# A hybrid decoder layer with product-key experts: ScalarE's reads of finished sums are put behind its casts, and three PSUM pools change size

## The chip, the cores and the metric

The kernel runs on one core of one Trainium2 chip. The metric is device microseconds (us) of one execution; before the change it is 3959.79 us, the median of three runs (3953.78 to 3965.73).

## The reference

One decoder layer of width 2048 for 512 tokens: two mixers side by side, then a feed-forward stage of experts. Nearly everything that the change touches lies in the experts:

```python
def one_block(xb):                                    # PEER_BLOCK tokens
    q = (xb @ w_query).reshape(PEER_BLOCK, 8, 2, 128)
    s = einsum('lhpd,hpnd->lhpn', q, sub_keys)
    s_half, i_half = top_k(s, 16)                     # 16 of 128 keys in each half
    ...                                               # 16x16 candidates, the best 16 of them
    gates = softmax(top_s)
    u = u_emb[eidx]                                   # 128 experts of 16384 for a token
    act = gelu(einsum('ld,lhkd->lhk', xb, u))
    return einsum('lhk,lhkd->ld', gates * act, v_emb[eidx])
```

The layer adds this, times a gate, to its input and ends with an RMS norm. Inputs and result are float32.

## The kernel before, in words

The mixers, their projections and the choice of experts take the first 1595 us. The experts take the rest, in two ways at once.

**Dense, for tokens 0 to 319** (`TD`). All 16384 experts are computed, and a table of gates is zero for those a token did not choose. `expert_u(i)` (L1158) computes 128 experts' scores: two pieces of 8 weight tiles go through `project_to` (L352), then ScalarE reads the finished sum `mm` from PSUM with a Gelu into `act` (L1162). `expert_g(grp)` (L1174) multiplies four of these by their gates on VectorE (L1188). `expert_v(grp)` (L1207) multiplies by the second table, in eight pieces with two sums `po` each, which VectorE adds into `hT` (L1228). There are 128 u's and 32 groups of v's.

**Gathered, for tokens 320 to 511** (`TG`). GpSimd's indirect DMA (`gather`, L1246) fetches each token's 128 rows of either table. VectorE multiplies and sums the u rows (`use`, L1259, L1263). The v rows are summed on TensorE by `part()` (L1274), here called a gathered sum: four matmuls into one PSUM tile `pw` (L1277), which ScalarE copies to `ys` (L1280) and a DMA of SyncE stores.

Float32 products are made of three matmuls (`mm3`, L204): high by high (L205), high by low (L206), low by high (L207). `split` (L199) makes the two parts of a piece: ScalarE casts the high part (L201; tiles `whi`, `vhi`, `ghi`), and GpSimd or VectorE subtracts it for the low part (L202; `wlo`, `vlo`, `glo`). The pieces of u and v share five raw buffers and three buffers each of high and low parts. So ScalarE has two kinds of work in one queue that is served in order: casts, which GpSimd and TensorE wait for, and reads of PSUM (Gelu, `ys`), which wait for TensorE.

From 1595 to 2003 us the gate table is made as well (`gate_block`, L1133): ten blocks of eight quarters. For a quarter VectorE makes `J` (L1140), VectorE and ScalarE make four `I` (L1146, L1149, L1150), TensorE multiplies them into a bank of `pg` (L1151), ScalarE copies the bank to `gb` (L1152). A block's eight copies fill the one buffer `gb`, which a 2 MB DMA stores.

PSUM has eight banks. From 1595 us on: `pu` (sums `mm`) 2, `pw2` (`pw`) 1, and 5 for `pg`, later for `pv` (sums `po`).

The order of the instructions is set when the program is built. The Python code emits them, a scheduler that simulates the engines then chooses an order by priority and readiness, and `tc.issue_after(x)` adds that what is emitted inside comes after instruction x. `pace` (L1194) uses this to space the gathers; a finished gather's `part` waits in the list `parts` until `project_to` or `expert_v` takes one between its matmuls.

Of the kernel before, what the change touches and what calls it, by code (L numbers as in the profile page):

```python
# [10 lines left out]
F32 = mybir.dt.float32  # L11
# [3 lines left out]
AF = mybir.ActivationFunctionType  # L15
OP = mybir.AluOpType
PSUM = bass.MemoryType.PSUM
DRAM = bass.MemoryType.DRAM

P = 128  # L20
T = 512
# [5 lines left out]
TD = 320  # L27
# [3 lines left out]
TF = 64  # L31
# [6 lines left out]
NSP = 36  # L38
# [98 lines left out]
def _hybrid(st, tc, nc, I, out):  # L137
    V, S, G, TE = nc.vector, nc.scalar, nc.gpsimd, nc.tensor
# [54 lines left out]
    eend = cp.tile([P, 64], F32, name="eend")  # L193

    copied = []
    parts = []
    done_mm = [None]

    def split(hi, lo, src, eng=None):  # L199

        copied.append(S.copy(hi, src))  # L201
        return (eng or V).tensor_tensor(lo, src, hi.bitcast(F32), OP.subtract)  # L202

    def mm3(ps, whi, wlo, xhi, xlo, first, last):  # L204
        TE.matmul(ps, lhsT=whi, rhs=xhi, start=first, stop=False)  # L205
# [36 lines left out]
    with ExitStack() as sb:  # L242
# [116 lines left out]
        def project_to(pss, ws, xhi, xlo, ahead=(), step=4):  # L359

            nk = ws.shape[2]
            ahead = list(ahead)
            for q in range(0, nk, step):
                n = min(step, nk - q)
                for j, ps in enumerate(pss):
                    whi, wlo, last = ahead.pop(0) if ahead else load_split(ws[j], q, n)
                    for i in range(n):
                        k = q + i
                        mm3(ps, whi[:, i, :], wlo[:, i, :], xhi[k], xlo[k], k == 0, k == nk - 1)
                        if parts and i % 4 == 3:  # L370
                            parts.pop(0)()
            return last

# [9 lines left out]
        with ExitStack() as s1:  # L383
# [158 lines left out]
            for n, (kind, i) in enumerate(MAMBA):  # L542
                ps = project(mm1, (kind, i), () if n else ahead)
# [406 lines left out]
    wp = st.enter_context(tc.tile_pool(name="wx", bufs=NSPL, reuse_waits="tile"))  # L950
    nraw = NRAW
    pu = st.enter_context(tc.tile_pool(name="pu", bufs=2, space=PSUM, reuse_waits="tile"))
    pw2 = st.enter_context(tc.tile_pool(name="pw2", bufs=1, space=PSUM, reuse_waits="tile"))
    npl = st.enter_context(tc.tile_pool(name="n2", bufs=1, reuse_waits="tile"))
    nhi = [npl.tile([P, TD], F32R, name=f"n2hi{k}") for k in range(KT)]
    nlo = [npl.tile([P, TD], F32R, name=f"n2lo{k}") for k in range(KT)]
# [1 line left out]
    gt_st = ExitStack()  # L958
# [7 lines left out]
    yG = dp.tile([TG, D], F32, name="yG")  # L966
# [6 lines left out]
    with ExitStack() as s3:  # L973
# [54 lines left out]
        for h in range(8):  # L1028
            sv = qp.tile([P, 2, 4, 16], F32, name="sv")
            si = qp.tile([P, 2, 4, 16], F32, name="si")  # L1030
            for hf in range(2):
                if h:
                    ps = pu.tile([P, T], F32, name="mm", tag="mm")
                    query([ps], 2 * h + hf)
                else:
                    ps = pss[hf]
# [72 lines left out]
        for src, dst in ((iall, iT), (jall, jT), (gall, gT)):  # L1109
            ps = pq.tile([P, 4, P], F32, name="sc")  # L1110
            for tt in range(4):
                TE.transpose(ps[:, tt, :], src[:, tt, :], ident)
            ps = ps.rearrange("p a b -> p (a b)")
# [9 lines left out]
    va = st.enter_context(tc.tile_pool(name="va", bufs=NACT, side="right", reuse_waits="tile"))  # L1123
    gr = st.enter_context(tc.tile_pool(name="gr", bufs=NGB, side="right", reuse_waits="tile"))
    gx = gt_st.enter_context(tc.tile_pool(name="gx", bufs=2, reuse_waits="tile"))
    pg = gt_st.enter_context(tc.tile_pool(name="pg", bufs=5, space=PSUM, reuse_waits="tile"))
    iota = gx.tile([P, P], F32, name="iota", bufs=1)
    G.iota(iota, pattern=[[1, P]], base=0, channel_multiplier=0, allow_small_or_imprecise_dtypes=True)

# [25 lines left out]
    acts = {}  # L1155
    actD = dp.tile([NSP, P, TD], F32, name="actD")

    def expert_u(i):  # L1158
        ps = pu.tile([P, T], F32, name="mm", tag="mm")
        last = project_to([ps[:, 0:TD]], I["uT"][i:i + 1], nhi, nlo, step=8)  # L1160
        acts[i] = va.tile([P, TD], F32, name="act")
        S.activation(acts[i], ps[:, 0:TD], AF.Gelu)  # L1162
        if i < NSP:
            nc.sync.dma_start(actD[i], acts.pop(i))
        return last

    ghl = {}
# [1 line left out]
    slots = []  # L1169
# [7 lines left out]
    def expert_g(grp):  # L1177
        gd = vp.tile([P, TD // TB, 4, TB], F32, name="gd", bufs=1)
        nc.sync.dma_start(gd, glD.rearrange("b j i t -> j b i t")[:, :, 4 * grp:4 * grp + 4, :])
        ghl[grp] = []  # L1180
        for i in range(4):
            n = 4 * grp + i
            if n < NSP:
                a = va.tile([P, TD], F32, name="act")
                nc.sync.dma_start(a, actD[n])
            else:
                a = acts.pop(n)
            V.tensor_tensor(a.rearrange("p (b t) -> p b t", t=TB), gd[:, :, i, :],  # L1188
                            a.rearrange("p (b t) -> p b t", t=TB), OP.mult)
            ghi = vp.tile([P, TD], F32R, name="ghi", bufs=7)  # L1190
            glo = vp.tile([P, TD], F32R, name="glo", bufs=7)
            split(ghi, glo, a, V)
            ghl[grp].append((ghi, glo))
# [14 lines left out]
    def expert_v(grp):  # L1208
        nonlocal nu
        gh = ghl.pop(grp)  # L1210
        for q in range(8):
            vr = wp.tile([P, 2, 4, P], F32, name="vr", tag="wr", bufs=NRAW)
            nc.sync.dma_start(vr, I["vq"][grp, q])
            vhi = wp.tile([P, 2, 4, P], F32R, name="vhi", tag="whi")
            vlo = wp.tile([P, 2, 4, P], F32R, name="vlo", tag="wlo")
            last = split(vhi, vlo, vr, G)
            po = [pv.tile([P, TD], F32, name="po") for _ in range(2)]
            for i in range(4):
                for d in range(2):
                    mm3(po[d], vhi[:, d, i, :], vlo[:, d, i, :], *gh[i], i == 0, i == 3)  # L1220
                if parts and i % 2:
                    parts.pop(0)()
            if grp == 31 and q % 2 == 0:
                sqs = vp.tile([P, 4, TD], F32, name="gd", bufs=1)
            for d in range(2):
                k = 2 * q + d
                h = hT[k]
                V.scalar_tensor_tensor(h, po[d], mod2[:, 48 + k:49 + k], h, OP.mult, OP.add)  # L1228
                if grp == 31:
                    t = sqs[:, k % 4, :] if k else sacc[:, 0:TD]  # L1230
                    S.activation(t, h, AF.Square)
                    if k:
                        V.tensor_tensor(sacc[:, 0:TD], sacc[:, 0:TD], t, OP.add)
            if q % 2 == 0:
                continue
            pace(last)
            if nu < min(128, 4 * grp + 8):
                pace(expert_u(nu))
                nu += 1
# [19 lines left out]
    def use(g, kind, i, n=None):  # L1259
# [14 lines left out]
        def part():  # L1274
            ps = pw2.tile([P, T], F32, name="pw")
            for q in range(4):
                TE.matmul(ps[32 * q:32 * q + 32, :], lhsT=wT[:, i:i + 1].to_broadcast([P, 32]), rhs=g[:, T * q:T * q + T],  # L1277
                          start=True, stop=True, tile_position=(0, 32 * q))
            ys = yp[-1].tile([P, T], F32, name="ys", bufs=len(yp))
            S.copy(ys, ps)  # L1280
            nc.sync.dma_start(yG[i].rearrange("(q n) -> q n", n=T), ys.rearrange("(q p) n -> q p n", p=32)[:, 0, :])
            held[0] -= 1
            if i % TF == TF - 1:
                late.extend((units + 2 + n, f) for n, f in enumerate(end_steps(i // TF)))

        parts.append(part)

# [49 lines left out]
    while nu < NSP:  # L1337
        pace(expert_u(nu))
        nu += 1
    gt_st.close()  # L1340
    pv = st.enter_context(tc.tile_pool(name="pv", bufs=5, space=PSUM, reuse_waits="tile"))
    vp = st.enter_context(tc.tile_pool(name="vp", bufs=2, side="right", reuse_waits="tile"))
    yp.append(vp)
    for grp in range(32):
        expert_g(grp)
        expert_v(grp)

    while slots or begun or parts or late:
        while parts:
            parts.pop(0)()  # L1350
        pace(done_mm[0])


# [30 lines left out]
```

## Time and profile before

| | |
|---|---|
| median of three runs | 3959.79 us |
| the profiled execution: its own time | 3952.57 us |
| its span | 3950.6 us |
| mean granted TensorE clock | 0.955 |
| TensorE busy | 3647.2 us, 92% |
| VectorE busy | 2431.9 us, 62% |
| ScalarE busy | 1454.1 us, 37% |
| GpSimd busy | 2429.3 us, 61% |
| DMA | 964.35 MB, mean 244 GB/s |
| chain that ended last, by engine | PE 66%, DVE 11%, POOL 7%, DMA 6%, issue 5%, ACT 1% |

PE is TensorE, DVE VectorE, ACT ScalarE, POOL GpSimd, SP SyncE. "Busy" is an average over stages that are bound by different things. "Idle before <-X" at an instruction is the time its engine stood still just before it, and X the instruction that ended that; idle time of an engine that others do not wait for costs nothing. Matmuls overlap: 0.31 us is one matmul's duration, and the distance of two starts tells the rate.

### The profile page before, as it was taken

The numbers are of one execution on the slowest core, as the hardware profiler recorded it, in microseconds if no ns is written. First come the engines' busy times: TensorE is split into PE (matmuls) and PEld (weight loads), VectorE is DVE, ScalarE is ACT, GpSimd is POOL, SyncE is SP. The second block draws the span as 40 slices with busy tenths as digits, with TensorE's granted clock in tenths as the row PEclk, the third lists the DMA queues.
The fourth block names the chain that finished last, engine by engine and source line by source line (L and its number), as shares of the span: only waits on it lengthen the run. The fifth ranks groups of instructions, "written<-read, shape, count | busy, mean of one in ns | idle before, by whom it ended". The sixth has DMA issues, their size and how long they took to land.

```text
span 3950.6 us, 61998 instructions
## 1 busy us (share of the span) xinstructions
PE 3647.2 (92%) x23708; PEld 3033.3 (77%) x23708; DVE 2431.9 (62%) x4440; ACT 1454.1 (37%) x2548; POOL 2429.3 (61%) x1393
## 2 busy tenths in 40 slices
PE   5899999999998899788979999999999999999998
PEld 3667757766666799787868788888888888788888
DVE  8543144556641699898768776657656666764225
ACT  3434323344322422565633333333333333333333
POOL 5445434433413655666647778777877887787765
PEclk8999999998888999898989999999999999999999
DMA  8465662324253422788779989898998989898884
GB/s 337 175 208 169 217 184 70 88 71 128 83 164 103 137 76 92 280 321 305 297 296 337 333 316 343 320 327 322 331 338 331 338 330 322 324 332 328 292 272 125
DMA packets 314007, 964.35 MB, mean 244 GB/s; under 512 B 67376, under 2 KB 132656, under 8 KB 257584
## 3 DMA queue, kind: packets, MB, share of 16 engines
q1 hardware_dynamic: 258416, 557.72, 42.1%
q0 software_dynamic: 55296, 402.68, 26.8%
q8 instruction: 187, 3.06, 0.3%
q14 instruction: 108, 0.88, 0.1%
HBM read 914.34 MB, written 45.94 MB: 243 GB/s over the span
## 4 chain that ended last, share of the span: by engine, by line
PE 66%; DVE 11%; POOL 7%; DMA 6%; issue 5%; ACT 1%; SPq 0%; POOLq 0%; DVEq 0%; ACTq 0%
PE mm L207 12%; PE mm L205 12%; PE mm L206 11%; PE po L207 6%; PE po L205 5%; PE po L206 5%; DVE g L1263 4%; PE pw L1277 3%; POOL vlo L202 3%; POOL wlo L202 2%; POOL g L1256 2%; DVE I L1146 2%; DMA AI<-abD 1%; PE pg L1151 1%; DVE act L1188 1%
## 5 line engine op out<-in xcount | busy, mean ns | idle before, releaser
L202 POOL TENSOR_TENSOR wlo<-wr,whi 128x1024 fp32r<-128x1024 f32 (+3 forms) x544 | 1051.5, 1940 | 797.2 <-ACT whi L201 710.2
L202 POOL TENSOR_TENSOR vlo<-vr,vhi 128x1024 fp32r<-128x1024 f32 x256 | 632.1, 2478 | 262.1 <-ACT vhi L201 257.2
L207 PE MATMUL mm<-n2hi,wlo 128*128 128x320 f32 x2304 | 732.9, 319 | 34.1 <-POOL wlo L202 33.9
L205 PE MATMUL mm<-n2hi,whi 128*128 128x320 f32 x2304 | 731.7, 318 | 11.8 <-ACT whi L201 8.4
L1263 DVE SCALAR_TENSOR_TENSOR g<-g,row 128x1024 f32<-128x1024 f32 x384 | 732.3, 1943 | 7.0 <-DMA g<-in_u,eix 3.9
L206 PE MATMUL mm<-n2lo,whi 128*128 128x320 f32 x2304 | 722.2, 314 | 0.2 <-DVE n2lo L202 0.2
L201 ACT CAST whi<-wr 128x1024 fp32r<-128x1024 f32 (+3 forms) x544 | 454.7, 840 | 671.7 <-PE mm L206 348.2
L205 PE MATMUL po<-ghi,vhi 128*128 128x320 f32 x2048 | 639.2, 317 | 35.7 <-DVE hT L1228 20.9
L206 PE MATMUL po<-glo,vhi 128*128 128x320 f32 x2048 | 637.2, 313 | 10.3 <-DVE glo L202 10.0
L207 PE MATMUL po<-ghi,vlo 128*128 128x320 f32 x2048 | 614.5, 317 | 20.9 <-POOL vlo L202 20.5
L207 PEld LDWEIGHTS mm<-n2hi,wlo 128*128 128x128 f32 x2304 | 438.4, 190 | 92.0 <-POOL wlo L202 64.0
L205 PEld LDWEIGHTS mm<-n2hi,whi 128*128 128x128 f32 x2304 | 439.9, 191 | 35.2 <-issue 18.2
L205 PEld LDWEIGHTS po<-ghi,vhi 128*128 128x128 f32 x2048 | 389.7, 191 | 83.4 <-issue 24.2
L206 PEld LDWEIGHTS mm<-n2lo,whi 128*128 128x128 f32 x2304 | 439.8, 191 | 4.2 <-issue 3.4
L1188 DVE TENSOR_TENSOR act<-gd,act 128x320 f32<-128x320 f32 x128 | 185.2, 1456 | 414.9 <-ACT act L1162 387.0
L207 PEld LDWEIGHTS po<-ghi,vlo 128*128 128x128 f32 x2048 | 380.3, 191 | 71.6 <-POOL vlo L202 45.5
L206 PEld LDWEIGHTS po<-glo,vhi 128*128 128x128 f32 x2048 | 391.2, 191 | 17.3 <-DVE glo L202 12.2
L1228 DVE SCALAR_TENSOR_TENSOR hT<-po,mod,hT 128x320 f32<-128x320 f32 x512 | 258.2, 544 | 234.6 <-PE po L207 220.6
L201 ACT CAST vhi<-vr 128x1024 fp32r<-128x1024 f32 x256 | 267.7, 1048 | 269.6 <-PE po L206 126.2
L1256 POOL DMA_INDIRECT g<-in_u,eix x192 | 237.8, 1239 | 78.3 <-issue 27.3
L1256 POOL DMA_INDIRECT g<-in_v,eT x192 | 224.8, 1171 | 70.1 <-issue 27.8
L205 PE MATMUL mm<-nhi,whi 128*128 128x512 f32 x640 | 261.8, 409 | 4.5 <-ACT whi L201 4.5
(448 smaller groups left out, 5839.6 us busy)
## 6 DMA issues: line engine op xcount, KB each, us to landing
wr<-in_uT SPq DMA_DIRECT2D x256, 512.0 KB
vr<-in_vq SPq DMA_DIRECT2D x256, 512.0 KB
wr<-in_wrest SPq DMA_DIRECT2D x160, 256.0 KB
aw<-in_ada SPq DMA_DIRECT2D x32, 1024.0 KB
a2w<-in_adar SPq DMA_DIRECT2D x64, 512.0 KB
glD<-gb SPq DMA_DIRECT2D x10, 2048.0 KB
gd<-glD SPq DMA_DIRECT2D x32, 640.0 KB
a3w<-in_adar SPq DMA_DIRECT2D x32, 512.0 KB
```

Source lines behind the costliest of these rows:

```text
L201: copied.append(S.copy(hi, src))
L202: return (eng or V).tensor_tensor(lo, src, hi.bitcast(F32), OP.subtract)
L205: TE.matmul(ps, lhsT=whi, rhs=xhi, start=first, stop=False)
L206: TE.matmul(ps, lhsT=whi, rhs=xlo, start=False, stop=False)
L207: done_mm[0] = TE.matmul(ps, lhsT=wlo, rhs=xhi, start=False, stop=last)
L1146: V.tensor_scalar(I2, iota, iT[:, t:t + 1], gT[:, t:t + 1], OP.is_equal, OP.mult)
L1151: TE.matmul(ps[:, i], lhsT=J[:, i], rhs=I2, start=True, stop=True)
L1188: V.tensor_tensor(a.rearrange("p (b t) -> p b t", t=TB), gd[:, :, i, :], a.rearrange("p (b t) -> p b t", t=TB), OP.mult)
L1228: V.scalar_tensor_tensor(h, po[d], mod2[:, 48 + k:49 + k], h, OP.mult, OP.add)
L1256: G.indirect_dma_start(out=g, out_offset=None, in_=I[s[0]], in_offset=bass.IndirectOffsetOnAxis(ap=ix, axis=0))
L1263: V.scalar_tensor_tensor(g[:, c], g[:, c], 1.0, n2s[i][:, c], OP.mult, OP.mult, accum_out=wtp[:, e, n:n + 1])
L1277: TE.matmul(ps[32 * q:32 * q + 32, :], lhsT=wT[:, i:i + 1].to_broadcast([P, 32]), rhs=g[:, T * q:T * q + T], start=True, stop=True, tile_p ...
```

## The change

Four edits, all in the experts. (1) The Gelu read and the copy to `ys` are no longer emitted at once: they go into a list `put_off`, and the next `split` whose low part is GpSimd's emits all of them, each ordered behind that split's cast. The store and the due end steps of `part` go along with its copy. The rests are emitted at the end of the gate stage, when `expert_g` needs an `act` that is missing, and in the last loop. (2) `project_to` takes a gathered sum after every eighth weight tile, not every fourth, and `expert_v` once in a piece, not twice. (3) `pw2` has two banks, not one. (4) `pg` and `pv` have four banks, not five. No instruction is added or removed; the choice of experts is as it was.

```diff
     copied = []
+    put_off = []
     parts = []
...
     def split(hi, lo, src, eng=None):
         copied.append(S.copy(hi, src))
-        return (eng or V).tensor_tensor(lo, src, hi.bitcast(F32), OP.subtract)
+        lo_ = (eng or V).tensor_tensor(lo, src, hi.bitcast(F32), OP.subtract)
+        if eng is G and put_off:
+            with tc.issue_after(copied[-1].ins):
+                while put_off:
+                    put_off.pop(0)()
+        return lo_
...
-                        if parts and i % 4 == 3:
+                        if parts and i % 8 == 7:
                             parts.pop(0)()
...
-    pw2 = st.enter_context(tc.tile_pool(name="pw2", bufs=1, space=PSUM, reuse_waits="tile"))
+    pw2 = st.enter_context(tc.tile_pool(name="pw2", bufs=2, space=PSUM, reuse_waits="tile"))
...
-    pg = gt_st.enter_context(tc.tile_pool(name="pg", bufs=5, space=PSUM, reuse_waits="tile"))
+    pg = gt_st.enter_context(tc.tile_pool(name="pg", bufs=4, space=PSUM, reuse_waits="tile"))
...
     def expert_u(i):
         ps = pu.tile([P, T], F32, name="mm", tag="mm")
         last = project_to([ps[:, 0:TD]], I["uT"][i:i + 1], nhi, nlo, step=8)
-        acts[i] = va.tile([P, TD], F32, name="act")
-        S.activation(acts[i], ps[:, 0:TD], AF.Gelu)
-        if i < NSP:
-            nc.sync.dma_start(actD[i], acts.pop(i))
+        def act():
+            acts[i] = va.tile([P, TD], F32, name="act")
+            S.activation(acts[i], ps[:, 0:TD], AF.Gelu)
+            if i < NSP:
+                nc.sync.dma_start(actD[i], acts.pop(i))
+
+        put_off.append(act)
         return last
...
             else:
+                while n not in acts:
+                    put_off.pop(0)()
                 a = acts.pop(n)
...
-                if parts and i % 2:
+                if parts and i == 3:
                     parts.pop(0)()
...
-            ys = yp[-1].tile([P, T], F32, name="ys", bufs=len(yp))
-            S.copy(ys, ps)
-            nc.sync.dma_start(yG[i].rearrange("(q n) -> q n", n=T), ys.rearrange("(q p) n -> q p n", p=32)[:, 0, :])
             held[0] -= 1
-            if i % TF == TF - 1:
-                late.extend((units + 2 + n, f) for n, f in enumerate(end_steps(i // TF)))
+
+            def out_of():
+                ys = yp[-1].tile([P, T], F32, name="ys", bufs=len(yp))
+                S.copy(ys, ps)
+                nc.sync.dma_start(yG[i].rearrange("(q n) -> q n", n=T), ys.rearrange("(q p) n -> q p n", p=32)[:, 0, :])
+                if i % TF == TF - 1:
+                    late.extend((units + 2 + n, f) for n, f in enumerate(end_steps(i // TF)))
+
+            put_off.append(out_of)
...
-    pv = st.enter_context(tc.tile_pool(name="pv", bufs=5, space=PSUM, reuse_waits="tile"))
+    pv = st.enter_context(tc.tile_pool(name="pv", bufs=4, space=PSUM, reuse_waits="tile"))
...
-    while slots or begun or parts or late:
-        while parts:
-            parts.pop(0)()
+    while slots or begun or parts or put_off or late:
+        while parts or put_off:
+            (put_off or parts).pop(0)()
         pace(done_mm[0])
```

Three places show what becomes of it in the order of the built program. The first is ScalarE's queue from the 60th Gelu of the experts on (near 2725 us before), where a gathered sum `ys`, a v piece `vhi` and a u piece `whi` meet; before:

```order
L1162 ACTIVATE act<-mm 128x320
L201 CAST ghi<-act 128x320
L1280 COPY ys<-pw 128x512
L201 CAST vhi<-vr 128x1024
L201 CAST whi<-wr 128x1024 x2
L1280 COPY ys<-pw 128x512
L201 CAST vhi<-vr 128x1024
```

and now:

```order
L1169 ACTIVATE act<-mm 128x320
L202 CAST ghi<-act 128x320
L202 CAST vhi<-vr 128x1024
L1294 COPY ys<-pw 128x512
L202 CAST whi<-wr 128x1024 x2
L1294 COPY ys<-pw 128x512
L202 CAST vhi<-vr 128x1024
```

The cast of the v piece has passed the copy of the gathered sum; the Gelu stands where it stood, with no cast moved ahead of it.

The second is TensorE's queue at the first gathered sum of the v groups (near 2031 us before), with the program's buffer numbers; `po_18851` and `po_18852` are the two sums of one piece. Before:

```order
L205 MATMUL po_18851<-ghi_18698,vhi_18847 128x320
L206 MATMUL po_18851<-glo_18699,vhi_18847 128x320
L205 MATMUL po_18852<-ghi_18698,vhi_18847 128x320
L206 MATMUL po_18852<-glo_18699,vhi_18847 128x320
L1277 MATMUL pw_18985<-g_18801,wT_11497 32x512 x2
L207 MATMUL po_18851<-ghi_18698,vlo_18848 128x320
L207 MATMUL po_18852<-ghi_18698,vlo_18848 128x320
```

and now:

```order
L211 MATMUL po_18851<-ghi_18698,vhi_18844 128x320
L212 MATMUL po_18851<-glo_18699,vhi_18844 128x320
L1288 MATMUL pw_18997<-g_18801,wT_11497 32x512 x4
L213 MATMUL po_18851<-ghi_18698,vlo_18845 128x320
L211 MATMUL po_18852<-ghi_18698,vhi_18844 128x320
L212 MATMUL po_18852<-glo_18699,vhi_18844 128x320
L213 MATMUL po_18852<-ghi_18698,vlo_18845 128x320
```

Two matmuls of the second sum no longer go ahead of the first sum's low product.

The third is ScalarE's queue in the gate stage, at the end of a block of the gate table (`whi` is the cast of a u piece, `I` the gate factors of the next block, numbered by the program). Before:

```order
L1150 ACTIVATE I_15154<-I_15154,gT,ngT 128x128
L1150 ACTIVATE I_15161<-I_15161,gT,ngT 128x128
L1149 ACTIVATE I_15172<-iota,iT 128x128
L1149 ACTIVATE I_15179<-iota,iT 128x128
L1150 ACTIVATE I_15172<-I_15172,gT,ngT 128x128
L1150 ACTIVATE I_15179<-I_15179,gT,ngT 128x128
L1152 COPY gb<-pg 128x128x4 x5
L1162 ACTIVATE act<-mm 128x320
```

and now:

```order
L1156 ACTIVATE I_15154<-I_15154,gT,ngT 128x128
L202 CAST whi<-wr 128x1024
L1155 ACTIVATE I_15161<-iota,iT 128x128
L1156 ACTIVATE I_15161<-I_15161,gT,ngT 128x128
L1169 ACTIVATE act<-mm 128x320
L1158 COPY gb<-pg 128x128x4 x4
L202 CAST whi<-wr 128x1024
L1169 ACTIVATE act<-mm 128x320
```

The copies of a block's first quarters stand together behind the store of the block before; before the change five quarters were made ahead of that point, now four (`I_15172` and `I_15179`, the fifth quarter's, come after the copies).

## Rows read from the trace of the kernel before

**Rows 1.** Windows by stage: start:end, length, busy of each engine, clock, DMA share, GB/s.

```profile
1595.00:2003.00 408.00, 355.31 (x2332) 334.16 (x2336) 334.04 (x437) 248.21 (x513) 256.81 (x128) 0.93 0.84 311
2003.00:2330.00 327.00, 293.26 (x1894) 256.33 (x1887) 258.60 (x313) 101.98 (x136) 229.99 (x122) 0.96 0.88 321
2330.00:3600.00 1270.00, 1200.84 (x7953) 1057.20 (x7952) 821.58 (x932) 416.07 (x561) 1007.83 (x526) 0.99 0.90 328
```

**Rows 2.** TensorE's waits, 2330 to 3600 us: total us, times, longest.

```profile
PE mm L207 <- POOL wlo L202: 31.5, 25, 1.6
PE po L207 <- POOL vlo L202: 19.7, 27, 3.2
PE po L206 <- DVE glo L202: 10.0, 4, 2.5
PE mm L205 <- ACT whi L201: 3.7, 9, 1.1
PE po L205 <- ACT vhi L201: 1.4, 4, 0.6
```

**Rows 3.** Timeline of ScalarE, 2724 to 2735 us: start, us, instruction, idle before.

```profile
2726.31 0.46 ACT L201 CAST ghi<-act 128x320 fp32r<-128x320 f32 x1 [0.56 <-DVE act L1188]
2728.98 0.59 ACT L1280 COPY ys<-pw 128x512 f32<-128x512 f32 x1 [2.21 <-PE pw L1277]
2729.46 1.05 ACT L201 CAST vhi<-vr 128x1024 fp32r<-128x1024 f32 x1
```

**Rows 4.** Timeline of GpSimd at the same place.

```profile
2730.59 2.37 POOL L202 TENSOR_TENSOR vlo<-vr,vhi 128x1024 fp32r<-128x1024 f32 x1 [6.44 <-ACT vhi L201]
```

**Rows 5.** Timeline of TensorE at the same place; the last row where it recurs.

```profile
2730.57 0.41 PE L205 MATMUL po<-ghi,vhi 128*128 128x320 f32 x1 [0.57 <-ACT vhi L201]
2730.96 0.31 PE L205 MATMUL po<-ghi,vhi 128*128 128x320 f32 x1
2731.11 0.31 PE L206 MATMUL po<-glo,vhi 128*128 128x320 f32 x1
2733.01 0.90 PE L207 MATMUL po<-ghi,vlo 128*128 128x320 f32 x2 [1.60 <-POOL vlo L202]
2733.71 0.47 PE L205 MATMUL po<-ghi,vhi 128*128 128x320 f32 x1
2733.98 0.47 PE L206 MATMUL po<-glo,vhi 128*128 128x320 f32 x1
...
3427.64 0.56 PE L207 MATMUL po<-ghi,vlo 128*128 128x320 f32 x2 [1.59 <-POOL vlo L202]
```

**Rows 6.** TensorE's waits, 1595 to 2003 us.

```profile
PE pg L1151 <- DVE I L1146: 32.6, 20, 4.2
```

**Rows 7.** VectorE's groups by line, 1595 to 2003 us: busy, mean ns, idle before.

```profile
L1146 DVE TENSOR_SCALAR I<-iota,iT,gT 128x128 f32<-128x128 f32 x160 | 119.4, 766 | 70.0 <-PE pg L1151 69.1
L1140 DVE TENSOR_TENSOR J<-iota,jT 128x512 f32<-128x512 f32 x79 | 63.2, 800 | 0.0
```

**Rows 8.** TensorE's waits, 2003 to 2330 us, then 3600 to 3840 us (the last row).

```profile
PE po L205 <- DVE hT L1228: 19.0, 11, 4.4
PE pw L1277 <- ACT ys L1280: 1.5, 2, 0.8
...
PE pw L1277 <- ACT ys L1280: 0.9, 1, 0.9
```

**Rows 9.** Waits of the whole span, VectorE for finished sums.

```profile
DVE hT L1228 <- PE po L207: 220.6, 133, 5.7
```

**Rows 10.** Timelines of VectorE (2355 and 2500 us on) and GpSimd: the product with the gates.

```profile
2358.61 0.48 DVE L1188 TENSOR_TENSOR act<-gd,act 128x320 f32<-128x320 f32 x1
2359.61 0.49 DVE L202 TENSOR_TENSOR glo<-act,ghi 128x320 fp32r<-128x320 f32 x1 [0.53 <-ACT ghi L201]
...
2509.19 3.40 DVE L1188 TENSOR_TENSOR act<-gd,act 128x320 f32<-128x320 f32 x1 [6.25 <-ACT act L1162]
...
2507.49 4.74 POOL L202 TENSOR_TENSOR vlo<-vr,vhi 128x1024 fp32r<-128x1024 f32 x2
```

More of the change, by code (lines that the diff above doesn't have):

```diff
@@ L1339, in _hybrid @@
         nu += 1
+    while put_off:
+        put_off.pop(0)()
     gt_st.close()
-    pv = st.enter_context(tc.tile_pool(name="pv", bufs=5, space=PSUM, reuse_waits="tile"))
+    pv = st.enter_context(tc.tile_pool(name="pv", bufs=4, space=PSUM, reuse_waits="tile"))
     vp = st.enter_context(tc.tile_pool(name="vp", bufs=2, side="right", reuse_waits="tile"))
```

## The prediction, made before the changed kernel ran

> **What bounds the kernel.** I read the windows by stage first, then TensorE's waits in each stage, then the timelines of the places where those waits lie. The windows [rows 1] say that TensorE is the bound in the experts, but not equally: in the gate stage (1595 to 2003 us) it is busy 355 of 408 us, in the first v groups 293 of 327, in the steady stage with u, v and gathers (2330 to 3600) 1201 of 1270. ScalarE, which the change is about, is busy 416 of 1270 us in the steady stage, so it has room; what can matter is only the order in which it serves its queue.
>
> What that order can cost is in TensorE's own waits of the steady stage [rows 2]: 31.5 us for `wlo`, 19.7 for `vlo`, 10.0 for `glo`, 3.7 for `whi`, 1.4 for `vhi`, together 66.3 us, 1.7% of the time. Not one of these rows ends at a DMA, although the DMA share is 0.90 [rows 1]. So 66.3 us is the most that an ideal order of casts could bring there. One place of the kind the change aims at is near 2727 us. ScalarE casts `ghi` at 2726.31, then stands 2.21 us until TensorE has a gathered sum, copies it at 2728.98, and only then, at 2729.46, casts the next v piece [rows 3]. GpSimd has stood 6.44 us for that cast and begins `vlo` at 2730.59 [rows 4]. TensorE waits 0.57 us for the cast and 1.60 us for `vlo` [rows 5].
>
> **The change, part by part.** I sum against the profiled execution's own 3952.57 us (its span is 3950.6); the median of the runs, 3959.79, is 7.2 us above it, and that is added at the end.
>
> *The later read.* The order of the built program decides what this does, and it hardly differs: a Gelu has as many casts ahead of it as before, since the scheduler had already let each read sink behind casts that were ready. At the 2727 us place the v cast now stands ahead of the copy. It can start when `ghi` ends, at 2726.77, and not at 2729.46: 2.7 us earlier, more than the 0.57 + 1.60 = 2.17 us that TensorE waits [rows 3, 5]. So I take all of 2.17 us away. The same pattern recurs once, near 3427 us, with the same 1.59 us row [rows 5]: 2 x 2.17 = 4.3. Behind the first of them the matmuls step by 0.27 us (2733.71 to 2733.98) where they stepped by 0.15 before (2730.96 to 2731.11), that is at the lower clock level after the idle time [rows 5]; nine such steps come back, 9 x 0.12 = 1.1. Elsewhere the order shows swaps of neighbours, as many for as against an earlier cast; I count them at nothing, between -33 us (half of the 66.3 gone, if ScalarE keeps ahead everywhere) and +5 us (two more places like the one removed). Nothing is near the first end in the order, so the sum takes **-5.4**.
>
> The deferral itself adds a wait: a Gelu behind a cast of 1.05 us [rows 3]. Behind it stand the gate product, `ghi` and `glo`, and the `mm` bank. I cost it at nothing, because the second `pu` bank takes the next u meanwhile; without that cover it would be 1.05 us for each of 128 u's, 134 us, but the leads in the order are unchanged, so there is nothing to cover.
>
> One rule speaks against an earlier `vlo`. The product with the gates takes 0.48 us when GpSimd stands still and 3.40 us when GpSimd is subtracting two `vlo` [rows 10], and each of the four waits for `glo` is about 2.5 us [rows 2]. The Trainium skill, "SBUF — State Buffer", section "Who interferes with whom", has the rule to it: a VectorE instruction with two inputs in SBUF contends with a GpSimd instruction that reads SBUF, and is blocked for as long as that runs. By it the two moved places would each pay 2.5 us for `glo`, and the sum would be 5.0 us higher. The rows near 2359 us, whose order on ScalarE is the one that the change brings to 2727, show `glo` done in 0.49 us [rows 10], before `vlo` starts; so I leave it out.
>
> *Fewer slots for gathered sums* move a `pw` group from the middle of a piece to its end. The four matmuls are the same. Nothing.
>
> *A second `pw` bank* removes TensorE's waits for the copy: 1.5 us in the first v groups, 0.9 at the end [rows 8]. **-2.4**. In the steady stage there is no such wait [rows 2], so nothing more.
>
> *Four banks for `po`.* The piece's second sum can start a little later. In TensorE's order two matmuls of it have stood ahead of the first sum's low products and no longer do: 2 x 0.147 = 0.29 us where TensorE waits for VectorE's addition, which it did 11 times [rows 8]: 11 x 0.29 = **+3.2**. The lower end is 0. The upper end: VectorE waited for a sum 133 times [rows 9]; the program has 256 pieces, so at up to 123 it was not ahead, 123 x 0.29 = +36.
>
> *Four banks for `pg`.* At the nine block ends of the gate stage one quarter less is made ahead. A quarter is 0.80 + 2 x 0.766 = 2.33 us of VectorE [rows 7]. VectorE is busy 334 of 408 us there and TensorE waits 32.6 us for its `I` [rows 1, 6], while VectorE waits 69.1 us for TensorE to free buffers [rows 7]: each is late for the other, so what is put off can be lost. Ends: 0, and 9 x 2.33 = +21.0. The order leaves 16 more gate matmuls, four quarters, behind the last u of the stage, 4 x 2.33 = 9.3 us of VectorE with no u beside it; but the u's stand that much earlier, so I take half, **+4.7**.
>
> Sum: -5.4 - 2.4 + 3.2 + 4.7 = +0.1. Own time 3952.7 us; against the median, **3959.9, say 3960 us: no change that can be measured**. What a measurement can tell from no change is 0.3%, 11.9 us.
>
> **The rivals.**
>
> *A, faster.* ScalarE, which is idle most of the time, uses the freedom: with the reads behind it and two `pw` banks it runs ahead of what the order suggests, and half of the 66.3 us goes, with nothing lost by the other pools. For it: the waits for `wlo` and `vlo` are 52 spread-out ones [rows 2], just what earlier casts would shorten. Against it: an engine works in its order, and that is nearly the old one. 3952.6 - 33.2 - 2.4 = 3917 own, 3924 by the median. Chance 0.18.
>
> *B, slower: the gate stage.* The lost `pg` bank costs its whole price at each block end, 21.0 in place of 4.7: 3952.6 - 7.8 + 3.2 + 21.0 = 3969 own, 3976 by the median. It decides, that is passes the 11.9 us, once over 16.5 us of the 21.0 are lost (16.5 - 7.8 + 3.2 = 11.9), at eight of nine ends. For it: both engines of that stage wait for each other [rows 6, 7]. Against it: `I` is late for want of VectorE, and a bank does not add VectorE time. Chance 0.16.
>
> *C, slower: the v pieces.* Each piece whose addition was not ahead loses its 0.29 us: 3952.6 - 7.8 + 4.7 + 36 = 3986 own, 3993 by the median. For it: 19.0 us of waits for `hT` before [rows 8]. Against it: all of them lie in 2003 to 2330 us, and the steady stage has none among its larger waits [rows 2]. The Trainium skill, "Perfetto Trace Analysis", section "Optimization Strategy", says that one gap repeating on the engine that should be saturated can mean that there isn't enough PSUM for the next tile; the trace of before shows no such gap on `po` in the steady stage with five banks, and no run here yet shows four. Chance 0.07.
>
> *D, the change does nothing:* order and waits stay, and the bank terms are nothing either; 3953 own, 3960 by the median. Chance 0.12; the time is the forecast's.
>
> **How the numbers follow.** The forecast has the remaining 0.47, of which 0.04 ends faster and 0.05 slower by over 0.3% through the ends of its own terms. Faster: 0.18 + 0.04 = 0.22. Slower: 0.16 + 0.07 + 0.05 = 0.28. Within: 0.38 + 0.12 = 0.50. The range reaches from 3936, which takes in the milder half of A, to 3988, which takes in B with the next mishap on top; left out are the stronger half of A and C, 0.16.
>
> **What would show it.** If the steps are right, the profile after has no `pw` waiting for `ys`; TensorE's 2.17 us near 2727 are gone; the steady stage's waits for casts and products sum to 58 to 67 us, against 66.3 [rows 2]; the gate stage is 0 to 9 us longer, with `pg` waiting for `I` up to 37 to 42 us; `po` waits for `hT` 20 to 24 us before 2330 and not behind it. I am wrong if the waits for `wlo` and `vlo` fall below 35 us together (A), if the gate stage is over 16 us longer (B), or if `po` waits for `hT` all through the steady stage (C).

## The result, and the profile after

The changed kernel takes 3913.84 us (median of four runs) against 3957.28 us before in the same rounds: ratio 0.9886, 95% interval 0.9867 to 0.9904, faster by 1.1%. In later rounds, beside other runs of before, it was 0.9913 (0.9894 to 0.9932). The forecast, no change, was wrong; so was its range, whose lower end was 3936. The profiled execution took 3915.02 us, its span 3912.9 us.

Where the time went is seen by cutting both spans at the same work: the end of the gate stage, the 37th Gelu of the experts and the 110th. The windows of the kernel after, columns as in [rows 1]:

```profile
1598.00:2005.00 407.00, 357.21 (x2343) 333.46 (x2344) 337.90 (x439) 249.28 (x512) 253.74 (x128) 0.94 0.84 312
2005.00:2323.00 318.00, 283.45 (x1850) 251.25 (x1850) 237.60 (x306) 100.21 (x134) 230.79 (x120) 0.96 0.90 328
2323.00:3565.00 1242.00, 1190.49 (x7973) 1053.78 (x7971) 797.54 (x937) 416.43 (x560) 1023.21 (x527) 1.00 0.91 335
3565.00:3867.00 302.00, 301.65 (x2079) 262.77 (x2078) 103.83 (x125) 111.91 (x154) 214.93 (x113) 1.00 0.80 281
```

and of the kernel before, cut at the same work:

```profile
2003.00:2325.00 322.00, 288.26 (x1860) 251.34 (x1853) 254.30 (x308) 100.15 (x133) 225.47 (x119) 0.96 0.88 322
2325.00:3598.00 1273.00, 1204.20 (x7976) 1061.58 (x7974) 824.71 (x937) 416.11 (x560) 1010.53 (x528) 0.99 0.90 328
3598.00:3905.00 307.00, 305.72 (x2083) 262.38 (x2082) 103.47 (x125) 114.62 (x155) 214.62 (x114) 1.00 0.80 277
```

The steady stage (third row above, second row here) has lost 31 us of the 37.7 by which the spans differ, with the same instructions in it; the first v groups and the last u's have each lost 4 to 5. I call "steady stage" this stretch of 73 u's from here on, 1273 us before. Of its 31 us, 17 were time in which TensorE stood still (the length less PE's busy time, 68.8 us before and 51.5 after), and 14 were busy time with the same matmuls, whose mean granted clock rose from 0.99 to 1.00. TensorE's waits in it, after:

```profile
PE mm L213 <- POOL wlo L203: 30.8, 26, 1.6
PE po L213 <- POOL vlo L203: 13.0, 17, 3.2
PE po L212 <- DVE glo L203: 4.1, 4, 1.0
PE mm L211 <- ACT whi L202: 1.8, 2, 1.3
```

Against [rows 2] the waits for `wlo`, the largest, have hardly moved. Those for `vlo`, `glo` and the casts have fallen from 34.8 to 18.9 us. VectorE's groups tell more. Before, then after (two fences, busy, mean ns, idle before):

```profile
L202 DVE TENSOR_TENSOR glo<-act,ghi 128x320 fp32r<-128x320 f32 x73 | 112.0, 1534 | 38.6 <-ACT ghi L201 35.7 <-ACT whi L201 2.9
L1188 DVE TENSOR_TENSOR act<-gd,act 128x320 f32<-128x320 f32 x73 | 100.2, 1372 | 253.5 <-ACT act L1162 244.1 <-DMA gd<-glD 9.4
```

```profile
L203 DVE TENSOR_TENSOR glo<-act,ghi 128x320 fp32r<-128x320 f32 x73 | 104.1, 1426 | 42.3 <-ACT ghi L202 42.3
L1199 DVE TENSOR_TENSOR act<-gd,act 128x320 f32<-128x320 f32 x73 | 74.9, 1026 | 226.6 <-ACT act L1169 226.6
```

The same 73 products with the gates take 25 us less of VectorE. The place where this begins is one that the prediction did not look at. Before, near 2416 us, the timelines of ScalarE, GpSimd and VectorE:

```profile
2416.28 0.59 ACT L1280 COPY ys<-pw 128x512 f32<-128x512 f32 x1 [6.04 <-PE pw L1277]
2416.77 1.05 ACT L201 CAST whi<-wr 128x1024 fp32r<-128x1024 f32 x1
...
2417.90 2.42 POOL L202 TENSOR_TENSOR wlo<-wr,whi 128x1024 fp32r<-128x1024 f32 x1 [3.81 <-ACT whi L201]
...
2422.68 4.74 POOL L202 TENSOR_TENSOR vlo<-vr,vhi 128x1024 fp32r<-128x1024 f32 x2
...
2424.37 3.41 DVE L1188 TENSOR_TENSOR act<-gd,act 128x320 f32<-128x320 f32 x1 [6.24 <-ACT act L1162]
2428.30 5.42 DVE L202 TENSOR_TENSOR glo<-act,ghi 128x320 fp32r<-128x320 f32 x1 [0.53 <-ACT ghi L201]
```

A copy of a gathered sum stands in ScalarE's queue ahead of a u piece's second cast and waits 6.04 us for TensorE. GpSimd waits 3.81 us for that cast, so its next subtractions, two `vlo`, run from 2422.7 to 2427.4. The next Gelu ends in that time, and VectorE's product takes 3.41 us in place of 0.48; `glo` then takes 5.42. After, the same work:

```profile
2407.81 1.05 ACT L202 CAST whi<-wr 128x1024 fp32r<-128x1024 f32 x1 [1.10 <-issue]
2412.75 0.59 ACT L1294 COPY ys<-pw 128x512 f32<-128x512 f32 x1 [3.89 <-PE pw L1288]
...
2408.15 4.74 POOL L203 TENSOR_TENSOR wlo<-wr,whi 128x1024 fp32r<-128x1024 f32 x2
...
2416.07 4.76 POOL L203 TENSOR_TENSOR vlo<-vr,vhi 128x1024 fp32r<-128x1024 f32 x2
...
2420.71 0.49 DVE L1199 TENSOR_TENSOR act<-gd,act 128x320 f32<-128x320 f32 x1 [5.11 <-ACT act L1169]
2422.49 2.31 DVE L203 TENSOR_TENSOR glo<-act,ghi 128x320 fp32r<-128x320 f32 x1 [1.29 <-ACT ghi L202]
```

The cast has passed the copy, the two `wlo` run without a gap, the two `vlo` are over at 2420.8, and the product takes 0.49 us. In ScalarE's order this swap ("whi, ghi, ys, whi" to "whi, ghi, whi, ys" behind a Gelu) stands at nine of the 73 u's, in twos and threes five u's apart; behind a tenth Gelu (the 77th) the cast passes the copy with `ghi` ahead of both casts.

What such a place costs depends on what TensorE needs next. Behind the one shown, the change gains 1.1 us. Behind another TensorE is at a v piece when `glo` is late: it is the place of [rows 10], with the product of 3.40 us. ScalarE's Gelus there and the matmul that waits for `glo`, before, and after with the product too:

```profile
2508.72 0.44 ACT L1162 ACTIVATE act<-mm 128x320 f32<-128x320 f32 x1 [3.27 <-PE mm L207]
2530.08 0.44 ACT L1162 ACTIVATE act<-mm 128x320 f32<-128x320 f32 x1 [5.96 <-PE mm L207]
...
2516.20 0.41 PE L206 MATMUL po<-glo,vhi 128*128 128x320 f32 x1 [2.50 <-DVE glo L202]
```

```profile
2504.01 0.44 ACT L1169 ACTIVATE act<-mm 128x320 f32<-128x320 f32 x1 [3.15 <-PE mm L213]
2521.76 0.44 ACT L1169 ACTIVATE act<-mm 128x320 f32<-128x320 f32 x1 [5.95 <-PE mm L213]
...
2504.48 1.30 DVE L1199 TENSOR_TENSOR act<-gd,act 128x320 f32<-128x320 f32 x1 [4.28 <-ACT act L1169]
...
2509.42 0.42 PE L212 MATMUL po<-glo,vhi 128*128 128x320 f32 x1 [1.01 <-DVE glo L203]
```

From Gelu to Gelu this u took 21.36 us before and 17.75 after. The wait for `glo` is 1.5 us shorter; and before, twelve matmuls behind the long wait stepped by 0.27 us, where the others step by 0.15 (granted clock 0.5, the lower of the two levels, 1.2 GHz, from 2517.5 to 2520.9 us). After, none does.

### The profile page after: what moved, and what is told of

It reads as the page before. It is cut to its first block, busy times and chain, and to the rows that moved or that the text cites. A ratio compares the mean times of both kernels' runs of the same rounds, so it can differ in the third digit from the quotient of the medians.

```text
span 3912.9 us, 62013 instructions
## 1 busy us (share of the span) xinstructions
PE 3632.4 (93%) x23708; PEld 3028.4 (77%) x23708; DVE 2388.3 (61%) x4440; ACT 1453.5 (37%) x2548; POOL 2445.0 (62%) x1393
## 4 chain that ended last, share of the span: by engine, by line
PE 36%; POOL 5%; DVE 3%; issue 3%; DMA 2%; ACT 1%; POOLq 0%; DVEq 0%; SPq 0%; ACTq 0%
PE po L213 7%; PE po L211 6%; PE po L212 6%; PE mm L213 5%; PE mm L211 5%; PE mm L212 4%; PE pw L1288 3%; POOL vlo L203 2%; POOL wlo L203 1%; POOL g L1267 1%; DVE g L1274 1%; DMA vr<-in_vq 1%; DVE glo L203 1%; DVE hT L1239 0%; DVE act L1199 0%
## 5 line engine op out<-in xcount | busy, mean ns | idle before, releaser
L1274 DVE SCALAR_TENSOR_TENSOR g<-g,row 128x1024 f32<-128x1024 f32 x384 | 710.3, 1886 | 7.7 <-DMA row<-n2D 4.1
L1199 DVE TENSOR_TENSOR act<-gd,act 128x320 f32<-128x320 f32 x128 | 155.1, 1221 | 385.3 <-ACT act L1169 364.6
L1267 POOL DMA_INDIRECT g<-in_u,eix x192 | 244.4, 1273 | 67.7 <-issue 28.5
```

Of the source, the lines that this page charges most:

```text
L1267: G.indirect_dma_start(out=g, out_offset=None, in_=I[s[0]], in_offset=bass.IndirectOffsetOnAxis(ap=ix, axis=0))
L1274: V.scalar_tensor_tensor(g[:, c], g[:, c], 1.0, n2s[i][:, c], OP.mult, OP.mult, accum_out=wtp[:, e, n:n + 1])
```

## The experiments

**Theory 1:** the swap starts GpSimd's subtractions earlier, so they no longer lie on VectorE's products; contention of the two engines (one slows the other) carries it to TensorE. **Theory 2:** the second `pw` bank. **Theory 3:** gathered sums no longer interrupt pieces. In the table, "steady" is the stretch of 73 u's in the one profiled execution, the start of the 110th Gelu less that of the 37th; ratios are to before, with their intervals. The kernels ran in several groups of rounds, each beside runs of before of its own, whose medians differ (3950.94 to 3957.28 us); so between groups the ratios compare, and the microseconds don't. The length of the steady stage repeats closely: two profiles of the changed kernel gave 1242.4 and 1242.8 us.

| | ratio | steady, us |
|---|---|---|
| before | 1 | 1272.9 |
| changed | 0.9886 (0.9867 to 0.9904) | 1242.4 |
| pools alone | 0.9991 (0.9972 to 1.0011) | 1277.1 |
| rarer places alone | 0.9962 (0.9950 to 0.9975) | 1272.8 |
| both later reads alone | 0.9933 (0.9914 to 0.9952) | 1246.4 |
| later copies alone | 0.9935 (0.9911 to 0.9958) | 1246.7 |
| later Gelu alone | 1.0013 (0.9992 to 1.0034) | 1273.8 |
| later reads and pools | 0.9907 (0.9886 to 0.9928) | 1243.1 |
| later copies and rarer places | 0.9913 (0.9892 to 0.9934) | 1249.0 |
| one SBUF input, reads at once | 0.9886 (0.9857 to 0.9914) | 1235.8 |
| one SBUF input, later reads | 0.9838 (0.9807 to 0.9869) | 1231.3 |

**The parts one by one.** First the pools:

```diff
-"pw2", bufs=1   "pg", bufs=5   "pv", bufs=5
+"pw2", bufs=2   "pg", bufs=4   "pv", bufs=4
```

> The kernel before with the pools of the change alone (pw 2 banks, pg 4, po 4). Theory 1 (the time went because the u piece's second cast now passes the copy of a gathered sum, which starts GpSimd's subtractions earlier and so keeps them off VectorE's gate product): that order is unchanged here, so the steady stage's waits for wlo, vlo and glo stay near 61 us and the time is within 8 us of before (3950 to 3965). Theory 2 (the second pw bank sets ScalarE and TensorE free): most of the gain is here, 3915 to 3930.

3949.21 us: just under theory 1's 3950, and not clear of no change. Theory 2's gain is not there. Then the rarer places:

```diff
-                        if parts and i % 4 == 3:
+                        if parts and i % 8 == 7:
...
-                if parts and i % 2:
+                if parts and i == 3:
```

> The kernel before with the rarer places for gathered sums alone. Theory 1: the order of casts and copies on ScalarE is unchanged, so 3950 to 3965, with the gate product near 1.4 us in the steady stage. Theory 3 (a gathered sum in mid-piece interrupts the matmuls, and that was the loss): 3915 to 3935.

3941.60 us: 0.38%, more than theory 1 allowed and less than theory 3 asked, and none of it in the steady stage. Then the later reads, with the rest as before:

```diff
-        acts[i] = va.tile([P, TD], F32, name="act")
-        S.activation(acts[i], ps[:, 0:TD], AF.Gelu)
...
+        put_off.append(act)
...
+            put_off.append(out_of)
```

> The later reads alone, with the pools and the places of gathered sums as before. Theory 1: the nine swaps of the u cast with the copy are here, so the steady stage gains its 25 to 30 us and the time is 3920 to 3935; the gate product's mean falls from 1.4 to near 1.0 us. Theories 2 and 3: within 8 us of before.

3927.23 us, the steady stage 26.5 us shorter, the product's mean 1.00 us: theory 1's numbers. With the pools added:

> The later reads and the pools, with gathered sums after every fourth tile and twice in a v piece as before. Theory 1: 3912 to 3925, a few us under the later reads alone for the second pw bank. Theory 3: within 10 us of before.

3920.83 us, inside theory 1's range.

**Which read.** The copies and the Gelu apart:

```diff
-        put_off.append(act)
+        act()
```

> The kernel before with only the copies of gathered sums put behind the next cast; the Gelu is emitted at once. Theory 1 (a copy that waits for a gathered sum no longer holds up the u piece's second cast): all nine swaps are in ScalarE's order, so the whole effect of the later reads is here: the steady stage 24 to 28 us shorter, 3925 to 3933. Rival (the later Gelu does it): within 8 us of before.

```diff
-            put_off.append(out_of)
+            out_of()
```

> The kernel before with only the Gelu put behind the next cast. Theory 1: no swap in the order, so within 8 us of before, the steady stage within 4 us of 1273. Rival: 3925 to 3935.

3932.79 and 3959.17 us. All of the later reads' gain is the copies'; the later Gelu does nothing that can be measured. Waits of GpSimd in the steady stage, with the later copies and then with the later Gelu (before: 51.7 us):

```profile
POOL wlo L203 <- ACT whi L202: 26.6, 14, 3.7
```

```profile
POOL wlo L203 <- ACT whi L202: 53.5, 21, 3.8
```

Not all of it is the u cast's. Taken from Gelu to Gelu, most u's of the run with both later reads last as long as before, within 0.05 us, and the rest add up to the 26.5 us: 20.9 lie at and just behind the ten u casts that pass a copy (1.1 us at each of six, 2.2 to 4.9 at each of the four behind which TensorE waited for `glo`), 6.0 at and behind the two places that the prediction named (near 2727 and 3427 us), and elsewhere 0.3 is lost.

**What carries it to TensorE.** To take the contention away, product and low part were made to read one SBUF tile and a constant PSUM bank; the gates and the true low part are left out:

```diff
+    one = pc.tile([P, T], F32, name="one")
+    V.memset(one, 1.0)
...
-            V.tensor_tensor(a.rearrange("p (b t) -> p b t", t=TB), gd[:, :, i, :],
-                            a.rearrange("p (b t) -> p b t", t=TB), OP.mult)
+            V.tensor_tensor(a, one[:, 0:TD], a, OP.mult)
...
-            split(ghi, glo, a, V)
+            copied.append(S.copy(ghi, a))
+            V.tensor_tensor(glo, ghi.bitcast(F32), one[:, 0:TD], OP.mult)
```

> Reads at once as before, four banks each for gate and v sums, and VectorE's gate product and the low part of it reading one tile from SBUF and a constant bank from PSUM (the gates and the true low part are left out). Theory 1 with contention as its medium: product and low part take about 0.5 us everywhere, so the steady stage is shorter than before's 1273 us by most of 30 us, 1240 to 1252, with the u cast still behind the copy. Rival (GpSimd's late subtraction reaches TensorE directly, contention or not): the steady stage stays above 1262 us.

> The same with the reads put behind the casts. Theory 1 with contention as its medium: the later reads have little left to gain, the steady stage within 8 us of the one with reads at once and one input. Rival: again 20 us or more shorter than that one.

With reads at once the steady stage fell to 1235.8 us; the later reads then gave 4.5 us in it, where they gave 26.5 with two SBUF inputs. (The 37 us against before are not contention's alone: the scheduler's order on ScalarE came out otherwise at 41 of the 73 u's.) VectorE's groups with reads at once, then the waits of GpSimd and of TensorE:

```profile
L1191 DVE TENSOR_TENSOR act<-one,act 128x320 f32<-128x320 f32 x73 | 35.7, 489 | 280.8 <-ACT act L1165 274.5 <-ACT whi L201 6.3
L1195 DVE TENSOR_TENSOR glo<-ghi,one 128x320 fp32r<-128x320 f32 x73 | 35.5, 487 | 63.6 <-ACT ghi L1194 53.2 <-ACT whi L201 7.9 <-issue 2.5
```

```profile
POOL wlo L202 <- ACT whi L201: 50.4, 21, 3.9
...
PE mm L207 <- POOL wlo L202: 23.4, 24, 2.0
PE po L207 <- POOL vlo L202: 10.1, 17, 1.5
```

With reads at once GpSimd still waits 50 us for casts that stand behind copies. The later reads halve that, to 24.9, as they do with two SBUF inputs, and it is worth little here: what mattered in the steady stage was where GpSimd's work fell. (These kernels' gate and v pools have four banks; the change's pools alone gave 1277.1.) Over the whole kernel the later reads still gave 15 us with one input (medians 3908.71 and 3893.69). The profiles show 5 us of that in the first v groups, beside the 4.5; where the rest lies is open, so this pair speaks for the steady stage alone.

**A version from this.** Gelu, product, cast and low part all work in the u's own PSUM bank, for u's 36 to 127, on top of the changed kernel:

```diff
+        if i % 4 == 0:
+            load_gates(i // 4)
+        m = ps[:, 0:TD]
+        S.activation(m, m, AF.Gelu)
+        gated(i, m)
...
+    def gated(n, a):
+        b = a.rearrange("p (b t) -> p b t", t=TB)
+        V.tensor_tensor(b, gdt[n // 4][:, :, n % 4, :], b, OP.mult)
...
+        split(ghi, glo, a, V)
```

> The changed kernel, with the gate product of u's 36 to 127 made in the sum's own PSUM bank (Gelu, product, cast and low part all read that bank), so that product and low part read one tile from SBUF each. Theory 1 with contention as its medium: both take near 0.5 us in the steady stage, which comes to 1231 to 1237 us as in the kernels that left the gates out; the time is 3898 to 3908, faster than the changed kernel's 3914. Rival (the bank held 1.5 us longer makes TensorE wait, or the one-input kernels gained from the missing gates): 3912 or more.

3894.32 us, ratio 0.9871 (0.9848 to 0.9894). The changed kernel had 0.9886 and 0.9913 in its two groups of rounds, with intervals that overlap this one, so the whole time alone does not settle that it is faster. The steady stage does: 1224.4 us, 18.0 less than in the changed kernel, with the same order on ScalarE at all 73 u's, and less than the 1231 to 1237 that was expected. Its groups and window:

```profile
L1198 DVE TENSOR_TENSOR mm<-gd,mm 128x320 f32<-128x320 f32 x73 | 36.1, 494 | 241.4 <-ACT mm L1175 241.4
L203 DVE TENSOR_TENSOR glo<-mm,ghi 128x320 fp32r<-128x320 f32 x73 | 35.8, 490 | 59.7 <-ACT ghi L202 53.7 <-ACT whi L202 2.7 <-issue 2.0
```

```profile
2321.00:3545.00 1224.00, 1185.50 (x7975) 1051.92 (x7978) 717.13 (x937) 411.89 (x561) 1026.95 (x527) 1.00 0.92 340
```

**A miss.** The waits for `wlo` that are left, 30.8 us, mostly come 1.2 to 1.6 us at a time; all 26 are at a subtraction that stands directly behind a gather in GpSimd's queue. So the gathers were emitted behind the next u:

```diff
-            pace(last)
             if nu < min(128, 4 * grp + 8):
-                pace(expert_u(nu))
+                after_u = expert_u(nu)
+                pace(last)
+                pace(after_u)
```

> The changed kernel, with a gather and the due uses emitted behind the u that follows, so that GpSimd takes the u piece's subtraction first. What is left of TensorE's waits for wlo is 30.8 us in the steady stage, most of it 1.42 us at a gather that stands ahead of a subtraction. If that gather is the cause: wlo waits under 15 us, and 3895 to 3905. If GpSimd's and VectorE's contention only moves: within 6 us of 3914.

> Both of these together. If the causes are apart: the sum of the two gains, 3882 to 3895. If both reach TensorE through the same late subtraction: no better than the better one.

3921.83 us (0.9932, 0.9909 to 0.9955) and 3909.01 us (0.9905): the first no faster than the changed kernel, the second slower than the PSUM version, in the same rounds. The waits for `wlo` became 32.4 us. But the edit hardly moved what it was to move: the gather still stands directly ahead of the subtraction at 25 of the 27 waits. One of them, GpSimd and then TensorE:

```profile
2359.98 1.77 POOL L1270 DMA_INDIRECT g<-in_v,eT  x1
2361.78 5.87 POOL L203 TENSOR_TENSOR wlo<-wr,whi 128x1024 fp32r<-128x1024 f32 x2
...
2364.35 0.42 PE L213 MATMUL mm<-n2hi,wlo 128*128 128x320 f32 x1 [1.26 <-POOL wlo L203]
```

So whether the gathers cause these waits stays open. The pair adds one thing: with the gathers emitted so, and again the same order on ScalarE, the PSUM product took the steady stage from 1245.7 to 1235.9 us and the median 12.8 us down.

**The remaining 0.4%.** Whether the parts add:

> The kernel before with the later copies of gathered sums and the rarer places for them, pools and Gelu as before. If the effects of the parts add (later copies 0.65%, rarer places 0.38%, pools 0.1% and not clear of zero): 3914 to 3920, the changed kernel's time without its pools. If the pools are needed for it: 3925 or more.

3911.68 us, ratio 0.9913: a little under what was expected, and with the old pools not to be told from the changed kernel. No need of the pools shows in the whole time. Then the rarer places for u pieces alone (only the first of the two edits above), and the gate sums' fifth bank given back, with a second bank for gathered sums only after the gate stage, in the changed kernel and in the PSUM version, all beside the changed kernel:

> The changed kernel again, beside the next three on the same chip. Ratio to before 0.987 to 0.990.

> The kernel before with rarer places for gathered sums inside u pieces alone; v pieces keep two. If what gains is the end of the gate stage, where the only gathered sums lie between u tiles: gate stage near 401 us and a ratio of 0.996 to 0.998. If the v pieces do it: gate stage 401 or 407, the first v groups 322 us, ratio 0.998 to 1.001.

> The changed kernel with five banks for gate sums and one for gathered sums up to the end of the gate stage, and four and two after it. If the fourth bank's loss in the gate stage is real (three pairs of kernels show 3 to 6.5 us there): gate stage 400 to 403 us and 3 to 7 us faster than the changed kernel. If not: gate stage 406 to 408 and the same time.

> The version with the gate product in the sum's PSUM bank and the mixed pools. If contention was what the changed kernel still lost and the gate bank another 3 to 7 us: 18 us from the steady stage and 3 to 7 from the gate stage, 20 to 25 us faster than the changed kernel beside it, ratio to before 0.981 to 0.985. If the earlier gain of that version was the chip's: within 8 us of the changed kernel.

The changed kernel gave 0.9913, slightly outside what was expected. The u places alone gave 0.9992 (0.9976 to 1.0008), not clear of no change and outside the interval of both edits together, so some of what the rarer places gain is the v pieces'. The profiles put the gain in two stages. The gate stage, from the first Gelu of the experts to its last matmul, took 407.5 us before, 401.2 with both edits and 400.8 with the u places alone. In the first v groups TensorE's waits for `hT` were, with both edits, then with the u places alone (before: [rows 8]):

```profile
PE po L205 <- DVE hT L1228: 14.7, 8, 4.4
```

```profile
PE po L205 <- DVE hT L1228: 18.6, 10, 4.3
```

and that stage, from the last gate matmul to the 37th Gelu, took 316.2 and 322.6 us, against 322.5 before. So the u places may be worth the 6 us of the gate stage, which their interval allows, and the v places the 6 us of the first v groups. That a gathered sum at a piece's end covers the wait for `hT` fits this, but no run took it apart. The mixed pools gave 0.9924 (0.9902 to 0.9946): no gain, and a new loss, the first v groups at 334 us; the PSUM version with them 0.9889 (0.9869 to 0.9908), 7 us under the changed kernel beside it and not 20 to 25, with the first v groups at 334 us as well. Against the mixed pools alone, which differ from it by the PSUM product only, its steady stage is 13.8 us shorter (1246.3 to 1232.5) and its median 11.6 us lower. Why mixed pools cost those groups 16 us was not followed up.

## Why the prediction was wrong

**The step that failed** is "Elsewhere the order shows swaps of neighbours, as many for as against an earlier cast; I count them at nothing". The count was wrong, and so was the price. As many for as against is what the timelines of ScalarE show for the Gelu, ten each way over the experts. But in the steady stage a cast has passed a copy 22 times and a copy a cast twice. Nine of these swaps are one and the same, a u cast that passes a copy, and the copy is a read that waits: at the place shown 6.04 us, where its own duration is 0.59. Taking swaps of neighbours as equal left out what each neighbour waits for. The later reads measured -26.5 us in the steady stage, where the sum had -5.4; the two places that it counted came in at -6.0, and the u casts that it counted at nothing at -20.9.

**The second failure** is the rule on contention. The row was read rightly (0.48 us alone, 3.40 beside GpSimd [rows 10]), and the Trainium skill, "SBUF — State Buffer", section "Who interferes with whom", says that a VectorE instruction with two SBUF inputs contends with a GpSimd instruction that reads SBUF. The one-input runs agree: 0.49 us on average, and none of the 73 above 0.50. But it was weighed only as a price of an earlier `vlo` and then left out. The long product of [rows 10] was there before the change, and an earlier subtraction shortened it (3.40 to 1.30 us): the four waits for `glo`, up to 2.5 us each [rows 2], became four of up to 1.0.

What held: the 2727 us place and the one near 3427, -6.0 us for the -5.4 of the sum. After the change that v cast follows `ghi` at once, and TensorE's two waits of [rows 5] are gone:

```profile
2716.14 0.46 ACT L202 CAST ghi<-act 128x320 fp32r<-128x320 f32 x1 [0.56 <-DVE act L1199]
2716.51 1.05 ACT L202 CAST vhi<-vr 128x1024 fp32r<-128x1024 f32 x1
2718.82 0.59 ACT L1294 COPY ys<-pw 128x512 f32<-128x512 f32 x1 [1.26 <-PE pw L1288]
```

The Gelu at nothing: held, 1.0013. The fewer slots at nothing: wrong by 0.38%, none of it in the steady stage. The second `pw` bank: -2.4 predicted, yet the waits for `ys` are still there in the first v groups (last row here; 1.5 before) and there are new ones at the end of the gate stage:

```profile
PE pw L1288 <- ACT ys L1294: 4.4, 4, 2.0
...
PE pw L1288 <- ACT ys L1294: 1.2, 1, 1.2
```

(first row: the whole span). The last u's, from the 110th Gelu to the 128th, did get 3 to 4 us shorter, and only in kernels with the second bank (302 to 303 us, against 305 to 306). Four banks for `po`, +3.2: not seen, `hT` waits 19.0 with the pools alone and 17.5 after. Four for `pg`, +4.7: the gate stage was 411 us with the pools alone against 407.5, but two profiles of the changed kernel itself gave 406.9 and 411.6, so single profiles can't settle a term of this size.

Rival A had the right sign and nearly the size (its 33 us; the steady stage lost 31), but the size was in part luck. It took half of the named waits away, and they fell by 17 us, from 66.3 to 49.7; the other 14 us were TensorE's busy time, as behind the long wait shown above. Nor did ScalarE run ahead of what the order suggests: the order itself had changed. Its test failed too: `wlo` and `vlo` together stayed at 43.8 us, above the 35 that were to mark it. Rivals B and C did not happen.

## What to carry to other kernels

When an order changes, look at each swap for what the passed instruction waits for, and follow the engine that waits behind it to where its work will now fall; one swap that recurs ten times (20.9 us) outweighed two places with a visible stall (6.0). A queue that mixes reads which wait for a slow producer with casts which others wait for should have the casts first; here that was worth 0.65%. Where two engines contend, a late start of one can show up as long instructions of the other: read the durations of one shape (here 0.49 to 3.41 us) before the waits, and give the instruction a PSUM operand if one is at hand.

## What was not expected of the hardware

VectorE's 128x320 product with both inputs in SBUF had a mean of 1.37 us in the steady stage before (36 of 73 over 1 us), and with one input in PSUM a mean of 0.49 and never over 0.50. The one at 2424.37 us, which began beside the first of two GpSimd subtractions in a row, ended 0.36 us after the second (2427.42 us), so it did not get in between them; the `glo` behind it was held for 5.42 us, over two subtractions of 2.4 us in a row. Where GpSimd paused for 0.21 us between two subtractions (near 2376 us), the product beside the first did get in: it took 1.13 us and ended 0.37 us after that first one. The addition into `hT`, which also reads one input from PSUM, took 544 ns on average in both kernels.
